# A three-level Strassen-Winograd mixture of experts on one core: P7 and P4 in stages of their own, P4 split a third time

## The chip, the cores and the metric

The kernel runs on one core of one Trainium2 chip. The metric is device time in microseconds (us) of one execution; lower is better. Times are the median of several executions. Beside them stands one execution taken with the hardware profiler, which gives the span of the program's instructions and the trace that all rows below come from.

## What is computed

Soft routing over eight experts: every token goes through every expert, and the results are added with the softmax of the router's logits as weights.

```python
probs = softmax(router_logits)                       # (16, 512, 8)
for e in range(8):
    output += probs[:, :, e:e+1] * (x @ expert_weights[e])   # x (16, 512, 512), W[e] (512, 2048)
```

With the weights of a token multiplied into its row of x this is one matrix product: 8192 tokens by (8 experts x 512) by 2048 output columns, in f32 outside. The kernel multiplies in f16 and sums in f32.

## The kernel before

**The outer level.** The 8192 rows are 32 blocks of 256 (`HQ`, line 55). Blocks 2q and 2q+1 (called a and b) make a pair, q = 0 to 15. The contraction is halved into experts 0 to 3 and 4 to 7, the output into two halves of 1024 columns. On these halves the kernel does a Strassen-Winograd product: seven products P1 to P7 for each q in place of eight. The right operands of P1 to P7 are sums of quarters of the expert weights; the left operands are sums of x times probabilities. `left_of` (line 671) says for each product which blocks of x (`xT` in the profile) and of the probabilities (`pT`) it needs, and `Left.make` (line 452) computes the left operand on VectorE, in two halves `k` (pairs of experts), each 128 x 2048 elements: a multiplication (`z<-xT,pT`), for P7 also a second multiplication of the other block (`u<-xT,pT`) and a subtraction (`z<-z,u`), for P6 a subtraction from P5's operand, and for most P3 a subtraction of a kept operand (`z<-z,w`). The kept operand is P6's left operand of the same q, which `keep_z` (line 1116) writes to DRAM (`z_dram`) while it is in use; `ZBlock` (line 494) loads it back, 1 MB, into a buffer of the weights' pool. `KEPT_Z = 14` (line 625): it is kept for q = 0 to 13, and P3 of q = 14 and 15 multiplies twice, like P7.

**The inner level.** Each product is itself a Strassen-Winograd product of halves (128 rows, one pair of experts, 512 columns): seven steps, in the order 1, 5, 6, 2, 7, 3, 4 (`STEPS`, line 353), each of eight matmuls of 128 x 128 by 128 x 512 (`Product.step`, line 572). A step needs the left operand's first half (steps 1, 5), second half (2, 4), a difference `d` (6) or the sum `i` (3, 7). After each step `post` (line 580) moves the result out of PSUM: alone (`post_alone`, mostly ScalarE copies) or on a base (`post_on_base`, line 606: VectorE adds the step's result to a 128 x 512 f32 tile `h` that holds what another product gave). `Base` (line 635) loads such tiles from DRAM; in `product` (line 696) P7's base is what P6 stored, and P4's base is P7's own tiles, `products[7, q].o`, still in SBUF. Each finished quarter of a product goes to the output by a DMA of GpSimd; P4 and P3 accumulate there (`accum_op=ADD`).

**The third level.** `by_thirds` (line 764) takes steps 1 and 5 of both products of a stage together and does them as one more Strassen-Winograd product: 2 x 7 parts of four matmuls of 128 x 128 by 128 x 256 in place of four steps of eight matmuls by 128 x 512. It needs sums of the two left operands (`Thirds.make`, four VectorE operations of 128 x 1024) and of the weights of steps 1 and 5 (`third_sums`, line 178, eight VectorE operations). Before the change it is used in stages 1 to 3 (P1) and 48 to 54 (P3).

**The order.** `add` (line 657) lines up stages of two products; a stage runs the steps of its two products by turns, and a slot is one step of one product. The list, by index: 0 to 14 P1 and P2; 15 to 30 P5 and P6 (16 alone); 31 (`k7`) P6 15 and P7 0; **32 to 46 P4 q with P7 q+1**; 47 (`k3`) P4 15 and P3 14; 48 to 54 pairs of P3; 55 P3 15.

`run` (line 827) walks through a stage slot by slot. Functions hung at (stage, slot) by `at` are called there: loads of bases (`fetch_at`), of weights (`turnover`, line 1096, on ScalarE's DMA queue), of kept operands (`load_z`, line 1122), and the preparation of P3's weights in four parts (`by_parts`). The other loads of a stage (x, probabilities, kept operands) are put on SyncE's (SP) queue two stages ahead, by `start_loads(stage + 2)` after slot `late.get(stage, 1)`: after the first slot of the stage unless `late` says otherwise; `late` has an entry for stages 46 and 47 only. The next stage's left operands join VectorE's list after slot `wait_for.get(stage, 1)`; they and the weights' sums are done between the additions on PSUM, as far as a cost model in the code (`slack`, line 384) sees room. All instructions of an engine run in the order in which they were issued, and so do the DMA issues of a queue; a DMA issue waits for its tile to be free and for the semaphore it will count on.

**Pools.** 15 buffers for weights and kept operands (8 KB a partition), 12 of 128 x 512 f32 (`h`), 10 for x and probabilities, 6 + 2 banks of PSUM (`ps`, `pt`).

Of the kernel before, what the change touches and what calls it, by code (L numbers as in the profile page):

```python
# [31 lines left out]
def kernel(  # L32
# [477 lines left out]
    class Thirds:  # L510


        def __init__(self, a, b, weights, room=None):
            self.a, self.b, self.weights, self.room = a, b, weights, room
            self.s, self.task = {}, None
# [109 lines left out]
    KEPT_Z = 14  # L625
# [45 lines left out]
    def left_of(r, q, fresh=True):  # L671
        a, b = 2 * q, 2 * q + 1
        if r == 1:
            pt = PBlock(a, P1, xp1[q - 2][1] if q in (2, 3) else None)
            if q in (2, 3):
                xs[a] = XBlock(a, xp1[q - 2][0])
            return Left(xblock(a), pt), [xblock(a), pt]
        if r in (2, 4):
            h, pt = (a, PBlock(a, P2)) if r == 2 else (b, PBlock(b, P2))
            return Left(xblock(h), pt), [xblock(h), pt]  # L680
        if r == 5:
            pt = PBlock(b, PQ)
            return Left(xblock(b), pt), [xblock(b), pt]
        if r == 6:
            pt = PBlock(a, P1)
            return Left(xblock(a), pt, of=lefts[5, q]), [xblock(a), pt]
        if r == 3 and q < KEPT_Z:
            pt, kept_z = PBlock(a, P2), ZBlock(q)
            return Left(xblock(a), pt, kept=kept_z), [xblock(a), pt, kept_z]
        pa, pb = PBlock(a, P1 if r == 7 else PQ), PBlock(b, P1 if r == 7 else PQ)  # L690
        return Left(xblock(a), pa, (xblock(b), pb)), [xblock(a), pa, xblock(b), pb]
# [4 lines left out]
    def product(r, q, **how):  # L696
# [18 lines left out]
        elif r == 6:  # L715
            m1 = bases[6, q]

            def base(tn):
                need(m1.task[tn])
                return m1.t[tn]  # L720
            p = Product(right[6], left, to_out(q, 0, 1), base)
        elif r == 7:
            base = bases[7, q] = Base(lambda tn: out_rows(q, 0, 1, tn))
            p = Product(right[7], left, to_out(q, 1, 1), base)
        elif r == 4:
            p = Product(right[4], left, to_out(q, 1, 0, accum_op=ADD), products[7, q].o.__getitem__)
        else:
            p = Product(right[3], left, to_out(q, 0, 1, accum_op=ADD), **how)
# [35 lines left out]
    def by_thirds(stage):  # L764
# [4 lines left out]
        place, keep = {}, {}  # L769

# [7 lines left out]
        for n, (p, r) in enumerate(((1, 1), (5, 1), (1, 5), (1, 6), (5, 6), (5, 5), (1, 2),  # L778
# [11 lines left out]
            if r == 1:  # L790
                keep[p] = half()
# [19 lines left out]
            elif r == 4:  # L811
                act(nc.scalar.copy(place["h", p][:, cols[0]], x))
                if p == 1:
                    some[1].post(1)
        for product in some:
# [58 lines left out]
    for q in range(15):  # L874
        add(product(4, q), product(7, q + 1))
    some = product(4, 15)
    xs.clear()
    k3 = add(some, product(3, KEPT_Z))
    for q in range(0, KEPT_Z, 2):
# [4 lines left out]
    products[4, 15].apart = True  # L884
# [9 lines left out]
    for q in range(16):  # L894
# [7 lines left out]
        for slot, tn in zip((7, 9, 11, 17), INNER):  # L902
            fetch_at(k7 + q - 1 + slot // 14, slot % 14, bases[7, q], tn)
# [187 lines left out]
    by_parts(k7 + 4, 4, 36, 3, cast_part(22), keep_raw, (9, 16))  # L1091
# [18 lines left out]
    turnover(k7, 0, 4, "t4")  # L1110
    turnover(k3 - 1, 1, 3, "b22", 2)

    for q in range(KEPT_Z):
# [8 lines left out]
    def load_z(q):  # L1122
        load = products[3, q].loads[-1]
        load.by_hook = True
        return load.begin
    at(k3 - 1, 10, load_z(0))
    at(k3, 2, load_z(1))
    third3 = {}

    def third_of_p3(p):  # L1130
        def make():
            third3[p] = third_sums(right[3].w[p])
        later(2.76, make)
    at(k3, 3, lambda: third_of_p3(1))
    at(k3, 5, lambda: third_of_p3(5))
    wait_for[k3] = 6
# [39 lines left out]
    for stage in range(k3 + 1, end):  # L1176
        thirds[stage] = Thirds(*(p.left for p in stages[stage]), third3, new_w)
# [42 lines left out]
```

## Time and profile before

| | us |
|---|---|
| median of 3 runs | 1367.95 |
| lowest and highest | 1367.74, 1368.5 |
| the profiled execution | 1368.82 |
| its span | 1367.0 |
| TensorE busy in it | 1359.6 |
| VectorE busy in it | 1124.8 |

PE in the profile is TensorE's matmuls and PEld its weight loads, DVE is VectorE, ACT ScalarE, POOL GpSimd, SP SyncE; SPq and ACTq are the DMA issues on those queues. A row of the groups gives line, engine, operation, the tile written and read, shapes and count, then busy time, the mean of one in ns, and the idle time before it with what ended it. A row of the timeline gives start, duration, and in brackets the idle time before it. A row of the windows gives a stretch, its length, the busy time (and count) of PE, PEld, DVE, ACT and POOL, the granted clock of TensorE as a share of full speed (1.00 throughout), the busy share of the DMA engines and the GB/s. A row of the DMA issues ends with the KB of one and the median us from issue to landing; a row of the DMA queues gives packets, MB and the share of sixteen engines' time (q0 is GpSimd's queue, q1 SP's, q10 ScalarE's). A matmul's record is longer than its pace: the records overlap.

### The profile page before, as it was taken

The page shows a single profiled execution, that of the slowest core. Times are in us where ns is not written, and L with a number is a line of the kernel's source. Part 1 is how long each engine was busy: PE and PEld are TensorE (multiplying, and loading weights), DVE is VectorE, ACT ScalarE, POOL GpSimd, SP SyncE. Part 2 cuts the span into 40 slices and gives each one's busy share as a digit, 9 for nine tenths or more (in the row PEclk, how much of TensorE's full clock was granted, in tenths as well). Part 3 has the DMA queues.
Part 4 walks back from the last instruction along what each step waited for, and adds up shares of the span by engine and source line. Part 5 has one row for each costly group of instructions (what it writes and reads, how often), then busy time and mean ns, then how long its engine had stood idle before and what let it go on. Part 6 is the DMA issues. An engine that isn't in the chain of part 4 may idle for free.

```text
span 1367.0 us, 18181 instructions
## 1 busy us (share of the span) xinstructions
PE 1359.6 (99%) x6630; PEld 645.4 (47%) x6630; DVE 1124.8 (82%) x1358; ACT 207.3 (15%) x397; POOL 411.8 (30%) x652
## 2 busy tenths in 40 slices
PE   9999999999999999999999999999999999999999
PEld 4555444444444444444444444444444444556554
DVE  7868767679789888788887888888889898898884
ACT  3232111100011111111111100000000000223331
POOL 3233233331223343333322112232332422233232
PEclk9999999999999999999999999999999999999999
DMA  9999999999899999999999998888897979999876
GB/s 185 207 246 233 229 254 255 244 294 385 252 309 273 334 343 317 292 277 316 309 302 324 322 399 240 199 237 208 231 265 203 259 184 298 328 306 240 189 122 127
DMA packets 193290, 360.09 MB, mean 263 GB/s; under 512 B 53168, under 2 KB 87216, under 8 KB 187696
## 3 DMA queue, kind: packets, MB, share of 16 engines
q0 software_dynamic: 88688, 185.12, 56.8%
q1 hardware_dynamic: 100480, 145.36, 35.4%
q10 hardware_dynamic: 4032, 28.44, 5.3%
q8 instruction: 52, 0.85, 0.3%
q14 instruction: 38, 0.31, 0.1%
HBM read 214.99 MB, written 171.11 MB: 282 GB/s over the span
## 4 chain that ended last, share of the span: by engine, by line
PE 97%; DMA 3%; POOL 0%; issue 0%; ACT 0%; DVE 0%; ACTq 0%; POOLq 0%; DVEq 0%
PE ps L130 71%; PE pt L130 25%; DMA h<-out_dram 2%; DMA w<-wd 1%; DMA w<-in_expert_weights_dram 1%; POOL w L121 0%; ACT h L614 0%; DVE ps L107 0%; ACT h L1168 0%; ACTq L164 0%; POOL ident L225 0%; POOLq L225 0%; DVEq L107 0%; POOLq L1204 0%
## 5 line engine op out<-in xcount | busy, mean ns | idle before, releaser
L130 PE MATMUL ps<-w,z 128*128 128x512 f16 (+1 forms) x3704 | 812.2, 376 | 0.8 <-DMA w<-wd 0.5
L130 PEld LDWEIGHTS <-z 128*128 128x128 f16 x5336 | 522.0, 98 | 606.2 <-issue 1.7
L121 POOL DMA_DIRECT2D out_dram<-h x380 | 248.8, 679 | 729.4 <-ACT h L614 337.0
L130 PE MATMUL pt<-w,z 128*128 128x512 f16 (+1 forms) x1632 | 357.7, 369 | 0.6 <-DMA w<-in_expert_weights_dram 0.5
L107 DVE TENSOR_TENSOR h<-ps,h 128x512 f32<-128x512 f32 x260 | 176.8, 686 | 120.9 <-PE ps L130 112.3
L107 DVE TENSOR_TENSOR z<-xT,pT 128x2048 f16<-128x2048 f16 x220 | 266.4, 1216 | 8.2 <-issue 7.2
L130 PE MATMUL ps<-w,d 128*128 128x512 f16 x880 | 199.1, 379 | 0.0
L107 DVE TENSOR_TENSOR h<-pt,h 128x512 f32<-128x512 f32 x155 | 105.7, 687 | 53.5 <-PE pt L130 46.7
L130 PEld LDWEIGHTS <-d 128*128 128x128 f16 x880 | 86.1, 98 | 101.7
L107 DVE TENSOR_TENSOR z<-z,d 128x2048 f16<-128x2048 f16 x110 | 132.4, 1215 | 0.0
L107 DVE TENSOR_TENSOR w<-w 128x1024 f16<-128x1024 f16 (+2 forms) x108 | 111.1, 1039 | 3.4 <-DMA w<-wd 1.7
L614 ACT COPY h<-ps 128x512 f32<-128x512 f32 x64 | 37.5, 586 | 486.2 <-PE ps L130 415.5
L601 ACT COPY h<-ps 128x512 f32<-128x512 f32 x90 | 52.7, 585 | 372.4 <-PE ps L130 316.0
L107 DVE TENSOR_TENSOR d<-z 128x1024 f16<-128x1024 f16 x110 | 74.6, 683 | 0.9
L107 DVE TENSOR_TENSOR ps<-ps,h 128x512 f32<-128x512 f32 (+1 forms) x86 | 54.0, 628 | 22.7 <-PE ps L130 18.6
L121 POOL DMA_DIRECT2D wd<-w x86 | 48.3, 585 | 41.6 <-DVE w L107 26.2
L121 POOL DMA_DIRECT2D w<-in_expert_weights_dram x65 | 48.9, 784 | 38.0 <-DMA wd<-w 28.1
L121 POOL DMA_DIRECT2D kept<-h x56 | 30.8, 550 | 60.2 <-DVE h L107 27.3
L597 ACT COPY h<-ps 128x512 f32<-128x512 f32 x65 | 36.7, 598 | 76.8 <-PE ps L130 67.3
L107 DVE TENSOR_TENSOR h<-h 128x512 f32<-128x512 f32 (+2 forms) x69 | 45.0, 674 | 0.6 <-ACT h L601 0.5
L107 DVE TENSOR_TENSOR z<-z,u 128x2048 f16<-128x2048 f16 x36 | 44.1, 1225 | 1.2
L107 DVE TENSOR_TENSOR u<-xT,pT 128x2048 f16<-128x2048 f16 x36 | 43.8, 1216 | 0.0
(72 smaller groups left out, 352.5 us busy)
## 6 DMA issues: line engine op xcount, KB each, us to landing
out_dram<-h POOLq DMA_DIRECT2D x380, 256.0 KB, 6.9
pT<-p_dram SPq DMA_DIRECT2D x126, 256.0 KB, 6.8
w<-wd ACTq DMA_DIRECT2D x27, 1024.0 KB, 9.7
h<-kept SPq DMA_DIRECT2D x100, 256.0 KB, 7.4
xT<-x SPq DMA_DIRECT2D x73, 256.0 KB, 6.7
wd<-w POOLq DMA_DIRECT2D x72, 256.0 KB, 7.5
w<-in_expert_weights_dram POOLq DMA_DIRECT2D x35, 512.0 KB, 10.5
h<-out_dram SPq DMA_DIRECT2D x68, 256.0 KB, 5.3
```

The costliest lines, as they stand in the source:

```text
L107: dve(nc.vector.tensor_tensor(out=o, in0=a, in1=b, op=op))
L121: note(nc.gpsimd.dma_start(out=o, in_=i, **how))
L130: note(nc.tensor.matmul(ps, z, w, start=start, stop=stop, skip_group_check=True))
L597: act(nc.scalar.copy(o[tn], q if p == 5 else x))
L601: act(nc.scalar.copy(o[TN[p]], b if p == 2 else x))
L614: act(nc.scalar.copy(o[tn], b))
```

## The change

P7 and P4 no longer share stages: 31 is P6 15 with P7 0, 32 to 38 are pairs of P7, 39 (`k4`) is P7 15 with P4 0, 40 to 46 are pairs of P4, 47 is P4 15 with P3 0, 48 to 54 pairs of P3 and 55 P3 15. The number of stages stays.

P4 loads its base from DRAM, from what P7 stored, instead of taking P7's tiles; the bases of both products of a stage are loaded at slots 8, 10 and 12 of the stage before and slot 3 of its own. Stages 40 to 46 use `by_thirds`; as their products lie on a base, the first addition of the second product is moved behind the split's last sum, and two temporary tiles (`keep`) come from the weights' pool.

P6's left operand is kept for all 16 q. P7 of q = 1 to 15 and all P3 use it: block b times its second probabilities minus the kept operand for P7. P7's kept operands of q = 1 and 2 are loaded at slots 0 and 2 of stage 31, as P3's of q = 1 and 2 at the same slots of stage 47; both stages have `wait_for` 6. P4's weights are loaded from stage 38 on, every second slot, instead of every third from stage 30 on; the preparation of P3's weights begins two stages earlier.

```diff
-        if r == 3 and q < KEPT_Z:
-            pt, kept_z = PBlock(a, P2), ZBlock(q)
-            return Left(xblock(a), pt, kept=kept_z), [xblock(a), pt, kept_z]
-        pa, pb = PBlock(a, P1 if r == 7 else PQ), PBlock(b, P1 if r == 7 else PQ)
+        if (r, q) != (7, 0):
+            h = a if r == 3 else b
+            pt, kept_z = PBlock(h, P2), ZBlock(q)
+            return Left(xblock(h), pt, kept=kept_z), [xblock(h), pt, kept_z]
+        pa, pb = PBlock(a, P1), PBlock(b, P1)
...
-            p = Product(right[4], left, to_out(q, 1, 0, accum_op=ADD), products[7, q].o.__getitem__)
+            base = bases[4, q] = Base(lambda tn: out_rows(q, 1, 1, tn))
+            p = Product(right[4], left, to_out(q, 1, 0, accum_op=ADD), base)
...
+        kept = left.keep and left.keep()
...
-                keep[p] = half()
+                keep[p] = half() if kept is None else kept.pop()
...
-                if p == 1:
+                if p == 1 and some[1].base is None:
                     some[1].post(1)
+            if (p, r) == (5, 3) and some[1].base is not None:
+                some[1].post(1)
...
-    for q in range(15):
-        add(product(4, q), product(7, q + 1))
+    for q in range(1, 15, 2):
+        xs.clear()
+        add(product(7, q), product(7, q + 1))
+    some = product(7, 15)
+    xs.clear()
+    k4 = add(some, product(4, 0))
+    for q in range(1, 15, 2):
+        xs.clear()
+        add(product(4, q), product(4, q + 1))
     some = product(4, 15)
     xs.clear()
-    k3 = add(some, product(3, KEPT_Z))
-    for q in range(0, KEPT_Z, 2):
+    k3 = add(some, product(3, 0))
+    for q in range(1, 15, 2):
         add(product(3, q), product(3, q + 1))
...
-        for slot, tn in zip((7, 9, 11, 17), INNER):
-            fetch_at(k7 + q - 1 + slot // 14, slot % 14, bases[7, q], tn)
+    fetch_base = zip((7, 9, 11, 17), INNER)
+    for slot, tn in fetch_base:
+        fetch_at(k7 - 1 + slot // 14, slot % 14, bases[7, 0], tn)
+    for r, q in [(7, q) for q in range(1, 16)] + [(4, q) for q in range(16)]:
+        k = {7: k7, 4: k4}[r] + (q + 1) // 2
+        for slot, tn in zip((8, 10, 12, 17), INNER):
+            fetch_at(k - 1 + slot // 14, slot % 14, bases[r, q], tn)
...
-    by_parts(k7 + 4, 4, 36, 3, cast_part(22), keep_raw, (9, 16))
+    by_parts(k7 + 2, 4, 36, 3, cast_part(22), keep_raw, (9, 16))
...
-    turnover(k7, 0, 4, "t4")
+    turnover(k4 - 1, 1, 4, "t4", 2)
...
-    for q in range(KEPT_Z):
+    for q in range(16):
         z_dram[q] = dram.tile([P, 2 * K8, HQ], f16, name=f"z_{q}")
...
-    at(k3 - 1, 10, load_z(0))
-    at(k3, 2, load_z(1))
...
-    at(k3, 3, lambda: third_of_p3(1))
-    at(k3, 5, lambda: third_of_p3(5))
-    wait_for[k3] = 6
+    for r, k in ((7, k7), (3, k3)):
+        at(k, 0, load_z(r, 1))
+        at(k, 2, load_z(r, 2))
+        wait_for[k] = 6
+    for r, k in ((4, k4), (3, k3)):
+        at(k, 3, lambda r=r: make_third(r, 1))
+        at(k, 5, lambda r=r: make_third(r, 5))
...
-    for stage in range(k3 + 1, end):
-        thirds[stage] = Thirds(*(p.left for p in stages[stage]), third3, new_w)
+    def keep_in_w():
+        t = wpool.tile([P, 4, NB], f32, name="keep", tag="w")
+        return [t[:, 0], t[:, 1]]
+    for r, first, to, keep in ((4, k4 + 1, k3, keep_in_w), (3, k3 + 1, end, None)):
+        for stage in range(first, to):
+            thirds[stage] = Thirds(*(p.left for p in stages[stage]), third_of[r], new_w, keep)
```

More of the change, by code (lines that the diff above doesn't have):

```diff
@@ L510, with __init__ @@
     class Thirds:
-        def __init__(self, a, b, weights, room=None):
-            self.a, self.b, self.weights, self.room = a, b, weights, room
+        def __init__(self, a, b, weights, room=None, keep=None):
+            self.a, self.b, self.weights, self.room, self.keep = a, b, weights, room, keep
             self.s, self.task = {}, None
@@ L624 @@
     QK = 9
-    KEPT_Z = 14
     ND = QK // 2
@@ L883 @@
     late[k3] = 10
-    products[4, 15].apart = True
     def claim(of, tn):
@@ L1120, with load_z, make_third @@
         at(k, 5, lambda keep_z=keep_z: keep_z(1))
-    def load_z(q):
-        load = products[3, q].loads[-1]
+    def load_z(r, q):
+        load = products[r, q].loads[-1]
         load.by_hook = True
         return load.begin
-    at(k3 - 1, 10, load_z(0))
-    at(k3, 2, load_z(1))
-    third3 = {}
-    def third_of_p3(p):
+    third_of = {4: {}, 3: {}}
+    def make_third(r, p):
         def make():
-            third3[p] = third_sums(right[3].w[p])
+            third_of[r][p] = third_sums(right[r].w[p])
         later(2.76, make)
-    at(k3, 3, lambda: third_of_p3(1))
-    at(k3, 5, lambda: third_of_p3(5))
-    wait_for[k3] = 6
+    for r, k in ((7, k7), (3, k3)):
[5 more added lines that the diff above has]
+        at(k, 5, lambda r=r: make_third(r, 5))
     finish = products[3, 15]
```

## The prediction, made before the changed kernel ran

> **What bounds the kernel now.** I read the head of the profile and the shares of its chain first, then the matmuls in order of time.
>
> ```profile
> span 1367.0 us, 18181 instructions
> ...
> PE 1359.6 (99%) x6630; PEld 645.4 (47%) x6630; DVE 1124.8 (82%) x1358; ACT 207.3 (15%) x397; POOL 411.8 (30%) x652
> ...
> PE 97%; DMA 3%; POOL 0%; issue 0%; ACT 0%; DVE 0%; ACTq 0%; POOLq 0%; DVEq 0%
> ```
>
> TensorE is busy for 99% of the span and makes 97% of the chain, so time is gained by fewer matmul columns and lost by holes between matmuls. I call the entries of `stages` by their index: 31 is (P6 15, P7 0), 32 to 46 the mixed pairs, 47 (P4 15 and a P3), 48 to 54 the P3 pairs with the third split.
>
> ```profile
> 828.24 3.62 PE L130 MATMUL pt<-w,z 128*128 128x512 f16 x16
> ...
> 852.41 3.62 PE L130 MATMUL pt<-w,z 128*128 128x512 f16 x16
> ```
> ```profile
> 1257.78 1.04 PE L130 MATMUL pt<-w,z 128*128 128x256 f16 x8
> ...
> 1281.16 1.04 PE L130 MATMUL pt<-w,z 128*128 128x256 f16 x8
> ```
>
> The first two rows are the same step of two successive mixed stages: 24.17 us for 14 steps of 8 matmuls, so 1.727 us a step (a slot, below) and 0.2159 us a matmul. The other two are the starts of two successive P3 stages with the third split: 23.38 us. Holes inside the part that changes:
>
> ```profile
> 796.01 7.07 PE L130 MATMUL ps<-w,z 128*128 128x512 f16 x32
> 802.92 3.62 PE L130 MATMUL pt<-w,z 128*128 128x512 f16 x16
> 806.37 3.62 PE L130 MATMUL ps<-w,d 128*128 128x512 f16 x16
> 809.83 5.34 PE L130 MATMUL ps<-w,z 128*128 128x512 f16 x24
> 815.49 1.89 PE L130 MATMUL ps<-w,z 128*128 128x512 f16 x8 [0.32 <-DVE h L107]
> 817.21 3.62 PE L130 MATMUL pt<-w,z 128*128 128x512 f16 x16
> 821.32 2.98 PE L130 MATMUL ps<-w,z 128*128 128x512 f16 x13 [0.49 <-DMA w<-wd]
> ```
>
> Twenty-four matmuls from 809.83 end at 815.01, but the next starts at 815.49 (0.48 late); sixteen from 817.21 end at 820.66, the next starts at 821.32 (0.66 late). That is 1.14 us in stage 32, where P4's weights arrive beside everything else. Two slots before 802.92 stage 32 begins: 799.47; stage 31 begins 14 slots earlier, at 775.29.
>
> **The change part by part.**
>
> *Third split of P4.* Stages 40 to 46 hold seven P4 pairs. If each runs like a P3 pair, TensorE saves 7 x (24.17 - 23.38) = **-5.53 us**. VectorE must follow:
>
> ```profile
> L107 DVE TENSOR_TENSOR z<-xT,pT 128x2048 f16<-128x2048 f16 x220 | 266.4, 1216 | 8.2 <-issue 7.2 <-DMA xT<-xs 1.0
> L107 DVE TENSOR_TENSOR z<-z,w 128x2048 f16<-128x2048 f16 x28 | 34.3, 1224 | 1.0
> L107 DVE TENSOR_TENSOR h<-ps,h 128x512 f32<-128x512 f32 x260 | 176.8, 686 | 120.9 <-PE ps L130 112.3
> L107 DVE TENSOR_TENSOR d<-z 128x1024 f16<-128x1024 f16 x110 | 74.6, 683 | 0.9
> ```
> ```profile
> 849.00:873.10 24.10, 24.10 (x113) 10.92 (x112) 20.43 (x24) 1.17 (x2) 5.60 (x9) 1.00 0.75 187
> 1257.78:1281.16 23.38, 23.38 (x137) 13.30 (x136) 20.55 (x26) 8.23 (x18) 7.28 (x9) 1.00 0.95 230
> ```
>
> (The fourth number of a row is VectorE's busy time, the last the GB/s.) A P3 pair multiplies and subtracts a kept operand (8 long operations); a P4 pair only multiplies (4), but its two products lie on a base: 12 adds of 0.686 us instead of 4. So -4 x 1.22 + 8 x 0.686 = +0.6 us on 20.55, under 23.38: no steady limit. PSUM's turn at the end of the split's fourteen parts gets one add of 0.69 us where P3 has a ScalarE copy; the next matmul on that bank is one part and one slot (0.43 + 1.73 us) away. I cost it at 0, and at up to 0.8 us a pair if the add comes late. The eight subtractions for P4's third weights (of `d`'s size, 0.68 each) fall in stage 39, with the four sums for stage 40's left operands and four long operations fewer than a mixed stage has: 20.43 + 12 x 0.68 - 4 x 1.22 = 23.7 of 24.17 us. Hidden, just.
>
> *P7 pairs.* A P7 had multiply, multiply, subtract for each half; now it has multiply and subtract of the kept operand. A stage of two P7 has 8 long operations, two `d`, two `z<-z,d` and 12 adds: as many as the mixed stage's 24 (20.43 us). Nothing on TensorE.
>
> *P4's weights leave stages 31 and 32.* They move to stages 38 and 39 with at least 13 slots between the last slot that gates each load and its use (22 us or more), as P3's weights have in stages 46 and 47, which show no hole. The 1.14 us goes: **-1.14 us**. What is late next is below.
>
> *DMA.* Rows of the page:
>
> ```profile
> out_dram<-h POOLq DMA_DIRECT2D x380, 256.0 KB, 6.9
> pT<-p_dram SPq DMA_DIRECT2D x126, 256.0 KB, 6.8
> w<-wd ACTq DMA_DIRECT2D x27, 1024.0 KB, 9.7
> ...
> h<-out_dram SPq DMA_DIRECT2D x68, 256.0 KB, 5.3
> ```
>
> A P7 stage now puts 14 transfers on SP: 2 `xT`, 2 `pT`, 8 bases (256 KB each) and 2 kept operands (1024 KB), 5.24 MB; with 8 stores (2.1 MB) and about 0.9 MB for P3's weights it moves 8.2 MB in 24.17 us, 340 GB/s. Stages of before that moved as much:
>
> ```profile
> 461.00:485.20 24.20, 24.20 (x113) 10.94 (x112) 21.87 (x29) 3.50 (x6) 10.33 (x20) 1.00 1.04 358
> 775.30:799.50 24.20, 24.20 (x114) 10.98 (x113) 21.24 (x26) 1.76 (x3) 4.32 (x8) 1.00 1.01 373
> 799.50:824.80 25.30, 24.49 (x114) 10.86 (x113) 20.27 (x24) 1.17 (x2) 5.41 (x8) 1.00 1.04 388
> ```
>
> 358 GB/s went without a hole; 388 had holes. In steady P7 stages bases are issued more than 13 slots ahead, so I cost them at 0. The Trainium skill, "DMA: Bandwidth & Descriptors", section Specifications, puts what HBM gives one core at about 358 GB/s. The third row is above it, so the measurement decides; by the rule the 24.2 us at 373 GB/s would take 25.2, 1 us more (an estimate).
>
> *Entry into P7 (stage 31): the new wait.* Stage 32 needs the kept operands z1 of (P7 1) and z2 of (P7 2). Their loads hang at slots 0 and 2 of stage 31, and between them stage 33's loads are put on SP at slot 1 (for stage 47 the code delays these to slot 10; for 31 nothing does). SP's order is z1, x, p, z3, x, p, z4, **z2**, bases. All of it stands behind a base that today goes out with the second of these:
>
> ```profile
> 770.30 5.27 SPq L118 DMA_DIRECT2D h<-out_dram  x2
> ```
> ```profile
> 782.98 0.58 ACT L601 COPY h<-ps 128x512 f32<-128x512 f32 x1 [17.26 <-DMA out_dram<-h]
> 783.00 2.22 ACTq L164 DMA_DIRECT2D w<-wd  x4
> ```
>
> So z1 goes out at about 775.5. z2 has one more gate: by the new program's waits it needs P7's sixth weight (step 3) landed. That load stands on ScalarE's queue behind the copy that a store holds until 783. Loads of that kind:
>
> ```profile
> w<-wd ACTq DMA_DIRECT2D x1, 1024.0 KB, 7.0
> ```
> ```profile
> w<-z SPq DMA_DIRECT2D x1, 1024.0 KB, 10.5
> ```
> ```profile
> q1 hardware_dynamic: 1224, 4.13, 51.1%
> ...
> w<-z SPq DMA_DIRECT2D x5, 1024.0 KB, 15.4
> ```
> ```profile
> w<-z SPq DMA_DIRECT2D x1, 1024.0 KB, 17.6
> ```
>
> The first row is the weight issued at 783 alone (a window around it). With z traffic beside it I take 8 us: landed, and z2 issued, at 791. A kept operand takes from 10.5 us (issued at 1165, little ahead of it) over a median of 15.4 (five of them between 1174 and 1197, `xT` and `pT` between) to 17.6 (issued at 1190.4). z2 has 2 MB of z3 and z4 and four small loads ahead, like the five; next to plain stores, not accumulating ones, I take 14.5. **z2 lands at 805.5** (801.5 to 808.6).
>
> Behind it VectorE has, in its order: subtract (1.22), three adds (0.69), `d` (0.68), multiply and subtract (2.44), two adds (1.38), some 7.8 us, 7.3 with the overlap seen between operations (24 operations of 21.8 us are 20.43 busy). The last of these adds frees the bank on which (P7 1) goes on in slot 4 of stage 32: 799.47 + 4 x 1.727 = 806.4. z2 would have to land by 799.1; it is 6.4 us late: **+6.4 us** (2.4 to 9.5). Bases queued behind z2 follow within the shifted time.
>
> And a stretch (1156 to 1166) with weights and kept operands on the way together, by queue, packets and MB:
>
> ```profile
> q10 hardware_dynamic: 296, 2.20, 57.6%
> q1 hardware_dynamic: 133, 1.04, 26.3%
> ```
>
> The same skill page, section Queues, rings and completion order, says that each DMA engine takes turns between the queues packet by packet; by it a kept operand would move at the pace of a weight, and z2 be nearer to the 10.5 us. The trace agrees in part only: the weights' queue (q10) moved 2.20 MB there, SP's (q1) 1.04.
>
> *Sum.* -5.53 - 1.14 + 6.4 = -0.3 us. The profiled execution took 1368.82 us around a span of 1367.0, 0.87 over the median of 1367.95; the difference carries over: 1367.95 - 0.3 = **1367.7 us**.
>
> **The rivals.**
>
> *The entry costs little* (faster). If z2 lands by about 802, stage 32 loses under 4 us, and the time is 1367.95 - 6.67 + (0 to 4) = 1361.3 to 1365.2. For it: 10.5 us is in the trace, and stage 47, with the same kind of entry, has no hole. Against: there z2's counterpart had one operand ahead of it, here three.
>
> *SP does not keep up in the P7 stages* (slower). They need 5.24 MB in 24.17 us from SP's queue, 217 GB/s. Between 1174 and 1197 that queue (q1) moved 4.13 MB in 23 us, 180 GB/s, while its loads queued up. It decides below 217: at 208 a stage takes 25.2 us, +1.0 for each of stages 32 to 38, and with the entry 1367.7 + 7 = 1375; at 180 it would be far more. Against: those stores accumulate, P7's do not, and the 358 GB/s row has no hole.
>
> *The split does not give P4 what it gives P3*: the add in place of the copy comes late in each pair, 0.8 us x 7 = 5.5 us, 1373.3. Against: VectorE's sum above.
>
> **How the numbers follow.** Forecast 0.47 (own range 1365.2, where the cheap entry begins, to 1370.8, z2 at its latest), entry cheap 0.27, SP too slow 0.20, split no gain 0.06. A measurement of this kernel tells about 0.2% (2.7 us) from no change, so the forecast is "within" (1365.2 to 1370.7): faster 0.27, same 0.47, slower 0.26. Range 1362.5 to 1374.5: below it lies the lowest part of the cheap entry (0.05), above it most of what a slow SP would be (0.13).
>
> **What would show it.** Right: stages 40 to 46 at 23.38 us; stage 32 stretched by 4 to 9 us with TensorE waiting for VectorE, and VectorE's subtraction waiting for DMA `w<-z` until about 805; no hole in stages 34 to 39. Wrong: stage 32 within 2 us of 24.17 (z2 in time), every P7 stage longer by the same amount (SP's rate), or P4 pairs at 24 us.

## The result and the profile after

The changed kernel takes **1378.79 us** (median of 6 executions, 1377.25 to 1383.66) beside 1368.14 of the kernel before (6 executions, 1367.74 to 1369.15): a ratio of 1.0082, 95% interval 1.0067 to 1.0098. It is 0.8% slower, and lies above the range of the prediction. The profiled execution took 1383.66 us, 4.9 over the median, so the holes below are probably somewhat larger than those of a usual execution.

The head, the chain and four DMA rows of the page after:

```profile
span 1381.9 us, 18753 instructions
...
PE 1361.0 (98%) x6798; PEld 663.5 (48%) x6798; DVE 1121.4 (81%) x1388; ACT 227.4 (16%) x453; POOL 411.7 (30%) x652
...
PE 71%; issue 15%; DMA 9%; POOL 5%; DVE 0%; SPq 0%; POOLq 0%; ACT 0%; ACTq 0%; DVEq 0%
...
out_dram<-h POOLq DMA_DIRECT2D x380, 256.0 KB, 7.8
h<-out_dram SPq DMA_DIRECT2D x132, 256.0 KB, 11.2
w<-z SPq DMA_DIRECT2D x31, 1024.0 KB, 14.0
...
w<-wd ACTq DMA_DIRECT2D x27, 1024.0 KB, 9.5
```

VectorE does no more than before, and TensorE's part of the chain fell from 97% to 71%. The base loads are 64 more, and one takes 11.2 us to land instead of 5.3. The times between the first matmuls of successive stages tell where the span grew. Each row below is a stage's length less 24.17 us (23.38 with the third split); what is not listed ran to within 0.3 us of that.

| kernel (profiled execution) | 31 | 32 | 38 | 39 | 43 | 46 | 47 | others |
|---|---|---|---|---|---|---|---|---|
| before | | 1.15 | | | | | | |
| after | | 5.74 | 1.18 | 7.79 | 2.16 | 4.17 | | |

The other stages with P4's split, 40 to 42, 44 and 45, last exactly 23.38 us, and 33 to 37 24.17. So the split gave what was forecast, and 21 us of holes took it back: 21.04 - 5.53 - 1.15 = 14.4 of the spans' 14.9; the other 0.5 lies ahead of stage 31, which the change does not touch.

TensorE's rows at the four large holes:

```profile
805.89 3.41 PE L130 MATMUL ps<-w,z 128*128 128x512 f16 x8 [4.06 <-DVE z L107]
```
```profile
995.32 5.97 PE L130 MATMUL ps<-w,z 128*128 128x512 f16 x16 [4.17 <-DVE h L107]
```
```profile
1093.34 10.53 PE L130 MATMUL ps<-w,z 128*128 128x512 f16 x48 [1.99 <-DVE z L107]
```
```profile
1161.08 3.29 PE L130 MATMUL ps<-w,d 128*128 128x512 f16 x8 [2.60 <-DVE ps L107]
```

It waits for VectorE each time, so the next view is what VectorE waited for: in stage 32 for the kept operand z2; in stages 38 (the first row of the second view), 39 (the next four) and 43 (the last two) for bases.

```profile
804.60 1.23 DVE L107 TENSOR_TENSOR z<-z,w 128x2048 f16<-128x2048 f16 x1 [9.55 <-DMA w<-z]
```
```profile
960.99 0.69 DVE L107 TENSOR_TENSOR h<-pt,h 128x512 f32<-128x512 f32 x1 [4.93 <-DMA h<-out_dram]
...
979.44 0.69 DVE L107 TENSOR_TENSOR h<-ps,h 128x512 f32<-128x512 f32 x1 [2.50 <-DMA h<-out_dram]
...
982.09 0.70 DVE L107 TENSOR_TENSOR ps<-ps,h 128x512 f32<-128x512 f32 x1 [0.82 <-DMA h<-out_dram]
...
985.05 0.70 DVE L107 TENSOR_TENSOR ps<-ps,h 128x512 f32<-128x512 f32 x1 [1.14 <-DMA h<-out_dram]
...
990.38 0.69 DVE L107 TENSOR_TENSOR h<-pt,h 128x512 f32<-128x512 f32 x1 [1.75 <-DMA h<-out_dram]
...
1087.61 0.69 DVE L107 TENSOR_TENSOR h<-ps,h 128x512 f32<-128x512 f32 x1 [1.15 <-DMA h<-out_dram]
...
1090.13 0.69 DVE L107 TENSOR_TENSOR h<-ps,h 128x512 f32<-128x512 f32 x1 [1.24 <-DMA h<-out_dram]
```

Stage 46 is another matter. VectorE first, then ScalarE and its queue:

```profile
1160.33 0.70 DVE L107 TENSOR_TENSOR ps<-ps,h 128x512 f32<-128x512 f32 x1 [3.54 <-DMA pT<-p_dram]
```
```profile
1159.51 0.33 ACTq L164 DMA_DIRECT2D w<-wd  x1
1159.94 0.63 ACT L814 COPY ps<-pt 128x256 f32<-128x256 f32 x2 [6.27 <-DMA xT<-x]
```

VectorE's row names a load of p, but that load was still on its way until 1163.0. What came just before 1160.33 was the first of the two ScalarE copies of line 814, which the split needs; the trace has VectorE's add wait for its semaphore. The copies stood 6.27 us behind a load of P3's weights on ScalarE's queue, and this load could be issued only when a load of x that counts on the same semaphore had landed (1159.5). No base is in that chain.

SP's queue around stages 38 and 39, first its own rows, then what its issues waited for from 925 to 1000 us (us in total, times, longest):

```profile
963.21 18.34 SPq L118 DMA_DIRECT2D h<-out_dram  x8
```
```profile
SPq L118 <- DMA h<-out_dram: 30.8, 13, 5.3
SPq L118 <- DMA out_dram<-h: 20.7, 5, 8.3
```

Eight base loads took SP 18.34 us to issue. It waited 20.7 us for stores to land (`out_dram<-h`: the tile `h` that a base is to fill still holds the result of an earlier step) and 30.8 us for base loads (the transfer before it on the same semaphore). And the loads, once issued, are slow; the DMA issues of stage 38:

```profile
h<-out_dram SPq DMA_DIRECT2D x6, 256.0 KB, 16.4
w<-in_expert_weights_dram POOLq DMA_DIRECT2D x4, 256.0 KB, 16.4
```

The second row is one of the four parts of P3's weights, cast from f32 on their way by GpSimd's queue, which begins in stage 38.

**Theory A** (on record for 46 as well): 12 tiles `h` do not suffice. Each base claims its tile from load to store, 8 tiles a stage; where landings are long, a store lands late, so the next base goes out late. **The rivals**: the third split's own order of additions makes the holes of 43 and 46 (C); the parts of P3's weights alone make those of 38 and 39 (G); SP or the DMA engines as a whole are full. Apart from it, stage 32 is the order on SP (E) or a gate that no order opens (F).

### The profile page after: what moved, and what is told of

The parts are those of the page before. It is cut to its first block, busy times and chain, and to the rows that moved or that the text cites. A ratio compares the mean times of both kernels' runs of the same rounds, so it can differ in the third digit from the quotient of the medians.

```text
span 1381.9 us, 18753 instructions
## 1 busy us (share of the span) xinstructions
PE 1361.0 (98%) x6798; PEld 663.5 (48%) x6798; DVE 1121.4 (81%) x1388; ACT 227.4 (16%) x453; POOL 411.7 (30%) x652
## 4 chain that ended last, share of the span: by engine, by line
PE 71%; issue 15%; DMA 9%; POOL 5%; DVE 0%; SPq 0%; POOLq 0%; ACT 0%; ACTq 0%; DVEq 0%
PE ps L130 53%; PE pt L130 17%; POOL out_dram L121 4%; DMA out_dram<-h 4%; DMA w<-in_expert_weights_dram 2%; DMA w<-z 1%; DMA w<-wd 1%; POOL wd L121 1%; DMA pT<-p_dram 1%; DMA wd<-w 0%; POOL w L121 0%; SPq L118 0%; POOLq L121 0%; DVE z L107 0%; DVE h L107 0%
## 5 line engine op out<-in xcount | busy, mean ns | idle before, releaser
L130 PE MATMUL ps<-w,z 128*128 128x512 f16 (+1 forms) x3760 | 823.9, 376 | 11.1 <-DVE z L107 6.0
L130 PE MATMUL pt<-w,z 128*128 128x512 f16 (+1 forms) x1520 | 322.7, 360 | 0.3 <-DMA w<-in_expert_weights_dram 0.3
L107 DVE TENSOR_TENSOR h<-ps,h 128x512 f32<-128x512 f32 x288 | 195.0, 687 | 125.9 <-PE ps L130 111.0
L107 DVE TENSOR_TENSOR h<-pt,h 128x512 f32<-128x512 f32 x127 | 86.4, 687 | 44.4 <-PE pt L130 32.8
L107 DVE TENSOR_TENSOR w<-w 128x1024 f16<-128x1024 f16 (+2 forms) x116 | 116.3, 1016 | 3.9 <-DMA w<-wd 2.1
L107 DVE TENSOR_TENSOR z<-z,w 128x2048 f16<-128x2048 f16 x62 | 76.0, 1225 | 12.0 <-DMA w<-z 10.0
L107 DVE TENSOR_TENSOR ps<-ps,h 128x512 f32<-128x512 f32 (+1 forms) x86 | 54.1, 630 | 27.3 <-PE ps L130 16.4
L130 PEld LDWEIGHTS <-w 128*128 128x128 f16 x528 | 49.2, 99 | 8.1 <-DMA w<-in_x_dram 1.5
## 6 DMA issues: line engine op xcount, KB each, us to landing
h<-out_dram SPq DMA_DIRECT2D x132, 256.0 KB, 11.2
```

The lines of the kernel that those rows point to most:

```text
L107: dve(nc.vector.tensor_tensor(out=o, in0=a, in1=b, op=op))
L130: note(nc.tensor.matmul(ps, z, w, start=start, stop=stop, skip_group_check=True))
```

## The experiments

Rows are profiled executions as above; the medians stand in the text, with the 95% interval of the ratio to the kernel before.

| kernel | 31 | 32 | 38 | 39 | 43 | 46 | 47 | others |
|---|---|---|---|---|---|---|---|---|
| stage 33's loads later | | 5.44 | 1.94 | 4.40 | 4.44 | 1.85 | | |
| no split of P4 | | 6.65 | 0.42 | 5.33 | | | | 48: 0.64 |
| P4 without base loads | | 7.25 | | 2.14 | | | | |
| 14 `h`, 8 for x | 7.62 | 1.17 | | 0.61 | | | | 2: 7.37, 10: 0.71, 20: 0.41 |
| 14 `h`, 10 for x | | 6.26 | | | | | 1.31 | 48: 0.76 |
| (P7 2) twice | 7.10 | 1.05 | | 6.36 | 5.68 | 1.45 | | |
| 14 `h`, (P7 2) twice | | 1.94 | | | | | 0.51 | 30: 0.60, 48: 0.76 |
| 14 `h`, order | | | | 1.62 | | | 1.12 | 20: 0.82, 48: 0.76 |
| 14 `h`, order, parts in 40 to 45 | | | | | | 12.83 | | 42: 10.89, 45: 5.50, 44: 2.07, 41: 1.51, 20: 0.92, 48: 0.47, 19: 0.38 |
| parts in 40 to 45 alone | | 6.95 | | | | 8.34 | | 42: 13.43, 45: 8.76, 41: 1.51, 44: 0.65, 48: 0.46 |
| before with 14 `h` | | 3.91 | | | | | | 26: 1.21 |
| 14 `h`, order, parts every 44 | | | | | | | 0.28 | 20: 1.80, 19: 0.95 |
| the same, P7's sums later | 4.10 | | | | | 2.72 | 3.45 | 22: 1.83, 21: 1.60, 30: 1.26, 26: 0.67 |

**1. Stage 33's loads behind z2.**

```diff
+    late[k7] = 10
```

> The changed kernel with stage 33's loads put on SP's queue at slot 10 of stage 31 instead of slot 1, so that z2 goes out ahead of z3 and z4. Theory A (the entry is late because z2 has three kept operands' worth of loads ahead of it on SP; the holes of stages 38, 39, 43 and 46 are another matter, the bases' cycle): stage 32's 5.7 us shrink to under 1.5, the other four stages keep their holes, 1373 to 1375 us. Rival (z2 is late because its weight gate opens late, whatever the order): stage 32 keeps over 4 us, 1377 to 1379. Rival (SP as a whole is behind in every P7 stage): what 32 gives back comes up in 33 to 38, 1378.

1381.66 us (1.0079 to 1.0109). z2 was in time now: the subtractions of kept operands ran at 794.99 and 800.17. But stage 32 kept its hole; VectorE waited for a base in place of z2:

```profile
812.99 1.37 DVE L107 TENSOR_TENSOR h<-pt,h 128x512 f32<-128x512 f32 x2 [7.53 <-DMA h<-out_dram]
```

The edit put z3 and z4 between the bases of slot 8 and those of slot 10. So it was not z2 alone: whatever stands behind those 2 MB is late. The other holes changed their sizes but not their places, and the median did not gain. My expectation of 1373 to 1375 failed.

**2. P4 without the third split.**

```diff
-    for r, k in ((4, k4), (3, k3)):
+    for r, k in ((3, k3),):
...
-    for r, first, to, keep in ((4, k4 + 1, k3, keep_in_w), (3, k3 + 1, end, None)):
+    for r, first, to, keep in ((3, k3 + 1, end, None),):
```

The first pair of lines takes out the sums for P4's third weights in stage 39 as well.

> The changed kernel without the third split of P4 (stages 40 to 46 do their 14 steps of eight matmuls; P4 still on a base from DRAM). Theory A (bases cycle): 40 to 46 cost 24.17 instead of 23.38, +5.5 us; the holes of 38 and 39 (9 us) stay, those of 43 and 46 (6.3 us) stay at over half, since the same bases, stores and weights move in nearly the same time: 1381 to 1384 us. Rival C (the split's order of adds and its temporary tiles make the holes of 43 and 46): both go, and 39 loses the part that third sums cost, 1374 to 1378.

1381.97 us (1.0082 to 1.0113). The holes of 43 and 46 went, as C has it; 39's stayed. The total is at A's number, though, since the saving of 5.5 went with them. This run alone does not tell C from A: without the split a stage is 0.8 us longer, and the base of a step is needed later after the stage's start. In 46 the copies of line 814 go with the split.

**3. P4 without base loads.** Zeros are added in place of P7's part, which is missing from that quarter of the output; the 64 loads are left out.

```diff
-            base = bases[4, q] = Base(lambda tn: out_rows(q, 1, 1, tn))
-            p = Product(right[4], left, to_out(q, 1, 0, accum_op=ADD), base)
+            p = Product(right[4], left, to_out(q, 1, 0, accum_op=ADD), lambda tn: nil.to_broadcast([P, NB]))
+            p.apart = True
...
-    for r, q in [(7, q) for q in range(1, 16)] + [(4, q) for q in range(16)]:
+    for r, q in [(7, q) for q in range(1, 16)]:
```

> The changed kernel with P4's 64 base loads taken out: VectorE adds a broadcast column of zeros instead, in as many additions of the same size, so that P7's part is missing from that quarter of the output. A base's buffer is then claimed at the first addition, not at the load. Theory A (base loads and their buffers): the holes of 43 and 46 go (6.3 us), and of 38 and 39 more than half (5 to 8 of 9 us), 1365 to 1368 us. Rival C (the split and VectorE's order): holes stay, 1377 to 1379. Rival D (weight turnover and P3's weights on the DMA engines in 38, 39 and 46): 43 goes, 39 and 46 stay at over half, 1372 to 1376.

1374.75 us (1.0031 to 1.0074), and above the expected 1365 to 1368, for stage 32 kept 7.25 us. With the split and as many additions, the holes of 38, 43 and 46 are gone: C falls for 43. (In 46 the copies ran 5.0 us after the stage's start, in after 9.5.) What is left in 39 is a P4 weight:

```profile
989.26 3.63 PE L132 MATMUL ps<-w,z 128*128 128x512 f16 x16 [1.24 <-DMA w<-wd]
```

**4. 14 tiles, taken from x.**

```diff
-    xpool = ctx.enter_context(tc.tile_pool(name="xpool", bufs=10))
-    hpool = ctx.enter_context(tc.tile_pool(name="hpool", bufs=12))
+    xpool = ctx.enter_context(tc.tile_pool(name="xpool", bufs=8))
+    hpool = ctx.enter_context(tc.tile_pool(name="hpool", bufs=14))
```

> The changed kernel with 14 tiles of 128x512 f32 for bases and results instead of 12, and 8 instead of 10 for x and probabilities. Theory A, buffer form (a base load waits until the store that used its buffer has landed): two more buffers are a quarter of a stage, 6 us, more lead: holes of 39, 43 and 46 (14 us) shrink to under 5, 1368 to 1371 us, if the loads of x keep up. Rival, DMA form (the loads go out in time and land late, since the DMA engines are full): holes stay within 2 us, 1377 to 1380; with x late too, more.

1377.38 us (1.0047 to 1.0081), above the 1368 to 1371 of the buffer form, which held only for the holes: from 38 to 46 all but 0.61 us went. Stages 2 and 31 lost 15 us instead; around 31 (765 to 825 us) SP waited for tiles that VectorE still read:

```profile
SPq L118 <- DVE z L107: 14.2, 4, 12.6
```

**5. 14 tiles, x left alone.** The 4 KB tile `u` is given up; its contents go through two `h` tiles, by halves.

```diff
-    hpool = ctx.enter_context(tc.tile_pool(name="hpool", bufs=12))
+    hpool = ctx.enter_context(tc.tile_pool(name="hpool", bufs=14))
...
-                u = new_u()
-                times(u, k, *self.less)
-                tt(t, t, u, SUB)
+                for e in range(2):
+                    u, half_ = h_tile([P, C, HQ], f16), t[:, ds(e * C, C)]
+                    tt(u, xb.t, pb.t[:, ds(2 * k + e, 1)].to_broadcast([P, C, HQ]), MUL)
+                    tt(half_, half_, u, SUB)
...
```

> The changed kernel with 14 tiles of 128x512 f32 and the 10 tiles for x and probabilities left as they are; the room comes from the separate 4 KB tile u, whose contents (GpSimd-stored weights, and the subtrahend of (P7 0)) now pass through two such tiles each, by halves. Theory A, buffer form: as with 14 and 8, the holes of 38, 39, 43 and 46 (15.3 us together) fall below 2, and stage 2 and 31 no longer wait for x; stage 32 keeps 5 to 7: 1364 to 1367 us. Rival (it was the delay at stage 31 by late x that spread the loads, not the buffers): holes of 39 to 46 come back at over 8 us, 1372 to 1378.

1369.65 us (0.9996 to 1.0015), 9 us under the changed kernel. From 33 to 46 no hole of 0.3 us is left: A is shown for 38, 39 and 43. (In 46 the copies ran 5.0 us after the stage's start, as in run 3.) The time stands 2.7 us above the expected 1364 to 1367: stage 32 lost what was expected, but 47 and 48 lost 2.07 us that were not. SP's waits from 925 to 1000 us:

```profile
SPq L118 <- DMA h<-out_dram: 21.7, 14, 3.8
...
SPq L118 <- DMA out_dram<-h: 4.3, 3, 3.4
```

Waiting for stores fell from 20.7 us to 4.3. How far ahead of its use a base goes out can be worked out from its issue and the slot that needs it (us, the eight bases of stage 39 in the order of their loads):

```
after      ahead  11.5 12.8 12.1 12.4  5.4  5.5  4.3  4.5   landing 15.4 17.9 17.2 19.4 14.8 14.8  4.7  3.8
14 tiles   ahead  23.9 21.2 19.7 21.0 20.7 21.0 22.5 23.3   landing 13.3 12.5 10.7 11.7 11.2 11.5 17.5 20.6
```

The landings are not much shorter. They are covered.

Why two tiles do so much can be worked out from the code. Tiles are taken in turn, so with 12 a base gets the tile of the twelfth base before it. For the third pair of a stage (slot 12; the fifth and sixth number of a row) that is the first pair of the stage before, which is stored after slots 6 and 7. The third pair is needed after slots 4 and 5 of its own stage, 12 slots or 20.7 us later, and between the two the store must land, the base go out, and the base land. In after this pair went out 0.1 us after that store had landed in each of stages 34 to 40 but 38. In stage 39 the stores took 10.1 and 8.9 us and the bases 14.8 each: 24.9 and 23.7 of 20.7 us. The other pairs have 18 slots, but stand in the same queue. With 14 tiles every pair has 20 slots, 34.5 us.

**6. and 7. (P7 2) multiplied twice, so that z2 is not loaded; alone and with 14 tiles.**

```diff
-        if (r, q) != (7, 0):
+        if r == 3 or q not in (0, 2):
...
-        at(k, 2, load_z(r, 2))
+        if r == 3: at(k, 2, load_z(r, 2))
```

> The changed kernel with (P7 2) multiplied twice instead of subtracting z2, so that stage 31 loads one kept operand for stage 32 and no wait for a weight's landing stands before the bases on SP. Theory E (the entry is late because everything on SP behind the weight-gated z2 and the 1 MB loads is late, bases included: taking z2 away brings the bases of stage 32 forward by the 9 us that SP stood): stage 32 loses under 2 us instead of 5.7, plus at most 1 for VectorE's longer list, 1374 to 1376. Rival F (the bases of stage 32 wait for stores and buffers anyway): stage 32 keeps over 4 us, 1377 to 1379.

> Both: 14 tiles as above and (P7 2) multiplied twice. Theory A with E: only small holes are left, 1360 to 1364 us, under the kernel before. Theory A with F (the entry stays): as the 14 tiles alone.

Alone 1381.08 us (1.0076 to 1.0108), above both expectations: stage 32 falls to 1.05, as E has it, but its hole comes up in stage 31, where a weight of P7 is late:

```profile
803.59 8.05 PE L130 MATMUL ps<-w,z 128*128 128x512 f16 x24 [5.28 <-DMA w<-wd]
```

With 14 tiles 1368.68 us (0.9992 to 1.0011). The profiled execution (1365.58) was its fastest; the median is 5 us over what was expected.

**8. 14 tiles, and stage 33's loads behind stage 32's bases.**

The edit stands on that of run 5.

```diff
...
+    late[k7] = 14
...
+    wait_for[k7 + 1] = 6
```

> 14 tiles as above, with z2 kept, stage 33's loads put on SP after slot 13 of stage 31, behind the bases of slots 8 to 12, and stage 33's left operands put on VectorE's list after slot 6 of stage 32. If the entry is a matter of order on SP alone, both z2 and the bases are in time and stage 32 loses under 2 us, but z3 and z4 come 20 us later than now and stage 33 may pay up to 3: 1360 to 1364. If the entry is set by the DMA rate (SP has 2 x 1 MB, weights and bases to move in the same 25 us in whatever order), stages 32 and 33 lose 4 to 7 together: 1364 to 1368.

1368.53 us (0.9988 to 1.0013). Stages 31 to 33 have no hole at all, against 6.26 us with 14 tiles alone: with 14 tiles the entry was a matter of order (E), of z2 and of the bases together, not of the DMA rate. The median still lies above the 1360 to 1364 that went with it. The executions spread from 1364.5 to 1372.0. In the profiled one 39 lost 1.62, with a P4 weight late by 1.44:

```profile
993.78 1.90 PE L130 MATMUL ps<-w,z 128*128 128x512 f16 x8 [1.44 <-DMA w<-wd]
```

A P7 stage of it, 34, as a window (columns as in the prediction), shows 395 GB/s beside a busy TensorE:

```profile
847.70:871.90 24.20, 24.20 (x114) 10.94 (x112) 21.75 (x27) 1.17 (x2) 6.99 (x13) 1.00 1.03 395
```

**9. and 10. The parts of P3's weights moved into stages 40 to 45; with all of 8, and alone.**

```diff
-    by_parts(k7 + 2, 4, 36, 3, cast_part(22), keep_raw, (9, 16))
+    by_parts(k4 + 1, 4, 16, 3, cast_part(22), keep_raw, (9, 16))
```

> 14 tiles and stage 33's loads behind stage 32's bases, as in the last run, and the preparation of P3's weights moved from stages 33 to 42 into stages 40 to 45 (every 16 slots from slot 4 of stage 40), where 240 to 290 GB/s were moved instead of 330 to 395. Theory A: the last hole of stages 38 and 39 (1.6 us, a P4 weight that lands late) goes, only 47 and 48 keep about 1.9, and with less traffic in 33 to 39 the executions scatter less: 1362.5 to 1365.5 us, under the kernel before. Rival (P4's own weights on ScalarE's queue are late for another reason): 39 keeps its hole, 1364 to 1368.5.

> The changed kernel with 12 tiles and its own order, and only the preparation of P3's weights moved to stages 40 to 45. Theory A (buffer cycle; the parts' traffic only lengthens the landings): 38 and 39 lose 9 us less 2 to 5, 43 and 46 gain nothing or lose 1 to 3 more: 1374 to 1380. Rival G (the parts in 38 and 39 are the cause of those holes): 38 and 39 under 1.5, 1369 to 1372.

1397.98 us (1.0184 to 1.0235) and 1406.26 us (1.0236 to 1.0289): far off. With a part begun every 16 slots, VectorE waited in its order for the store of a raw part, which its sums overwrite:

```profile
1068.28 2.87 DVE L107 TENSOR_TENSOR w<-w 128x1024 f16<-128x1024 f16 x4 [6.62 <-DMA wd<-w]
```

But the second kernel answers G, for 38 and 39. With 12 tiles and nothing else changed they have no hole, where A alone had 4 to 7 us left, and a base lands in 6.2 us instead of 16.4 (950.7 to 974.9, after's stage 38; this kernel's begins 0.8 us later):

```profile
DMA packets 2788, 8.37 MB, mean 346 GB/s; under 512 B 376, under 2 KB 376, under 8 KB 2409
...
h<-out_dram SPq DMA_DIRECT2D x8, 256.0 KB, 6.2
```

The same window of the changed kernel:

```profile
DMA packets 3411, 7.92 MB, mean 327 GB/s; under 512 B 352, under 2 KB 1367, under 8 KB 3091
...
q0 software_dynamic: 1512, 2.47, 46.7%
```

It moved less, at 327 GB/s, and a base took almost three times as long. So it was not the bytes: the casting loads made the landings long. They put 1015 packets of 512 B to 2 KB into the window that without them has none, and GpSimd's queue (q0) held the engines for 46.7% of the time to move 2.47 MB (without them 24.1% for 2.18); that it is the size of these packets is argued from this, not shown. Other stages of after agree: in 33 and 41, each with four casting loads, a base took 13.9 and 12.9 us, in 34 and 40, which moved more GB/s without them, 10.1 and 8.2.

The bases of this kernel's stage 39, as in the table of run 5, and one row of SP's waits from 925 to 1000 us:

```
parts late ahead  18.8 19.6 20.8 21.5 14.4 10.9 19.7 16.1   landing  6.2  6.0  6.2  6.0  8.5  8.5  8.9  4.3
```
```profile
SPq L118 <- DMA out_dram<-h: 45.3, 11, 8.2
```

SP waited more than twice as long for stores as in after (20.7 us), and nothing was lost: the wait of a queue is no cost as long as the lead that is left covers the landing. So it takes both to make the holes of 38 and 39, too few tiles and long landings, and either remedy is enough: short landings with 12 tiles, or 14 tiles with long ones. For 43, 14 tiles, no base loads, or the longer stage without the split each were.

**11. The kernel before with 14 tiles.** The same tiles and the same halves for `u`.

> The kernel before with 14 tiles in place of 12, u taken apart in the same way (a P7's subtrahend is made and subtracted by halves, four operations of 128x1024 in place of two of 128x2048). Theory A: it had no hole for want of tiles, so nothing is gained, and up to 1.5 us lost by VectorE's extra operations: 1367 to 1370. If tiles were short there too, its 1.4 us of holes go: 1366.5.

1372.52 us (1.0009 to 1.0034). More tiles bring the kernel before nothing; it loses 2.8 in stage 32 (3.91 for 1.15) and 1.2 in 26. That is more than I had expected. In stage 32 VectorE waited 5.13 us for a base (at 805.06); why that base was late stays open.

**12. 14 tiles, order, and the parts every 44 slots**, so that none begins in stage 38 or the first half of 39.

```diff
-    by_parts(k7 + 2, 4, 36, 3, cast_part(22), keep_raw, (9, 16))
+    by_parts(k7 + 2, 4, 44, 3, cast_part(22), keep_raw, (9, 16))
```

> 14 tiles, stage 33's loads behind stage 32's bases, and the four parts of P3's weights started every 44 slots from slot 4 of stage 33 instead of every 36, so that they start in stages 33, 36, 39 (slot 8) and 42 and none lies in stage 38 and the first half of 39, where P4's weights are loaded. Theory: the loads of 38 and 39 land some us sooner and the 1.6 us that 39 waited for a P4 weight go: profile with holes in 47 and 48 only, 1362.5 to 1365.5 us for the profiled execution, the median 1364 to 1368. Rival: the loads of the fourth part in 42 and 43 cost there what they cost in 39, 1367 to 1371; or stage 20 and other places outside the change, which showed holes of up to 0.9 with this set of tiles, decide the scatter, and the median stays at 1368.5.

**1365.79 us** (median of 11, 1363.91 to 1370.98), ratio 0.9983, 0.9973 to 0.9994: the one version that beats both kernels. Three windows of its profile, stages 31, 39 and 43, columns as in the prediction:

```profile
778.33:802.50 24.17, 24.17 (x113) 10.98 (x112) 20.18 (x25) 1.76 (x3) 4.32 (x9) 1.00 1.02 411
...
971.70:995.90 24.20, 24.20 (x114) 10.95 (x113) 22.53 (x32) 1.17 (x2) 8.33 (x12) 1.00 1.04 330
...
1066.03:1089.41 23.38, 23.38 (x138) 13.30 (x136) 21.14 (x29) 4.09 (x10) 8.57 (x11) 1.00 1.09 248
```

TensorE is busy throughout. From 31 to 46 there is no hole. The time came as expected, but not all of the mechanism: the holes that were left lay not in 47 and 48 but in 19 and 20, outside the change, 2.75 us. In 20 VectorE waited 3.96 us for a load that the sums of P7's weights need (at 530.66); in 19 it was busy up to the hole. Without the two the span would be 1361.0.

**13. The same, with those sums 10 slots behind their loads instead of 7.**

```diff
-    by_parts(k5 + 2, 4, 13, 7, load_part("t3"), None, (7,))
+    by_parts(k5 + 2, 4, 13, 7, load_part("t3"), None, (10,))
```

> As the last run, with the sums of P7's weights (stages 17 to 20) put on VectorE's list 10 slots after each part's load instead of 7. If the 2.75 us that stages 19 and 20 lost in the last run's profile are VectorE waiting for these loads, with additions that free TensorE's banks queued behind, both holes go: a profiled execution at 1361.5 to 1363.5 us, the median 1362 to 1365.5. The sum of the prediction's steps without an entry was 1361.3. Rival (the holes there are the cost of 14 tiles, whose base loads go out earlier and stand against the parts; they move to another wait): 19 and 20 lose over 1 us, 1364.5 to 1366.5.

1377.37 us (1.0033 to 1.0072; 1369.92 to 1379.29). The holes of 19 and 20 went and came back in 21 and 22, and the profiled execution had holes in 31, 46 and 47 that the run before had not. Why a shift in stages 17 to 20 is felt in 46 was not settled. The rival, that these holes move, was the nearer one, and even it was too low.

## Why the prediction was wrong, by its own steps

- **Third split, -5.53 us: right.** Seven stages of P4 at 23.38 us, in after those five without a hole, in run 12 all seven. The add in the copy's place cost nothing, and the sums for the third weights fit into stage 39 (run 12). The rival without a gain falls.
- **P7 pairs, nothing: right.** Stages 33 to 37 last 24.17 us.
- **P4's weights, -1.14 us and no new hole: half right.** The old hole went. "As P3's weights have in stages 46 and 47" did not hold: a P4 weight ended a wait of 1.24 us in run 3 and of 1.44 in run 8. In after itself no matmul waited for one: the bases were later. And P3's weights, the model for it, had a hole in stage 46 this time (below).
- **DMA, "bases are issued more than 13 slots ahead, so I cost them at 0": the step that failed.** In the profiled execution it should have been 11.1 us, the holes of 38, 39 and 43. I read the lead from the order of the program, where nothing holds SP's issue but its place. In the trace a base waits for the store that empties its tile: 13 slots are 22.5 us, and stage 39's bases went out 4.3 to 12.8 us ahead, with landings of up to 19.4. By the code the third pair's tile is stored only 12 slots, 20.7 us, before its use (run 5). With the page's medians, 6.9 us for a store and 5.3 for a base, that still looks like nothing; with the landings of a busy stretch it does not, and before's trace had one: of what was issued between 786 and 794 us, a store took 8.3 and a base 17.7 (medians), 26 us in all.
- **Stage 46, 4.17 us: a wait that the sum did not have.** The prediction looked at the split's turn on PSUM by VectorE's add alone, and took P3's weights in stage 46 as harmless, as they were before. With the split in 46, VectorE needs ScalarE's copies early in the stage, and these stand behind the weights' loads on ScalarE's queue. Run 1 shows the same: the copies waited 5.36 us there, and 46 lost 1.85.
- **The rival "SP does not keep up in every P7 stage": wrong in place and cause.** 33 to 37 had no hole, though they moved up to 364 GB/s, and stage 34 of run 8 moved 395 without one. The loss stood where landings were longest (the bases of 38 and 39 took 15.7 and 15.1 us, medians; those of the other stages from 32 to 46, 8.3 to 12.9) and in 43, one of the stages that the split shortens.
- **The rule on what HBM gives one core, weighed there:** the Trainium skill, "DMA: Bandwidth & Descriptors", section Specifications, about 358 GB/s. The trace disagrees: 411 over the 24.17 us of stage 31 in run 12, with TensorE busy throughout.
- **Entry, +6.4 us (2.4 to 9.5): right in size, right only in part in its mechanism.** 5.74 us, and z2 used at 804.60 where I had it landing at 805.5; the cheap entry, under 4, falls. The nearness to 6.4 is in part luck: z2 made TensorE 4.2 us late, and the other 1.5 are matmuls at half pace (below), which the sum did not have. And TensorE stopped already at slot 1, for the left operand of (P7 2) itself, not at slot 4 for a bank. Besides, the entry was no matter of z2 alone: with z2 early the bases behind it cost as much (run 1), with z2 gone a weight did (run 6).
- **Holes cost more than their length.** I priced a hole by its idle time. After three of after's four large holes TensorE went on at half pace, which is 5.1 of the 21 us (below).
- **What would show it:** the signs for the split and for stage 32 came as written; against "no hole in stages 34 to 39" spoke 38 and 39, and for 43 and 46 no sign had been named.

The gains were forecast at 6.67 us. Run 12 shows them without most of the holes: its span of 1363.7 less 3.0 of holes against 1367.0 less 1.4 (1.15 in stage 32, 0.26 in 49) is a gain of 4.9, and before's hole of 1.15 in stage 32 is gone as well, 6.1 together. What turned the sum were the holes of 38, 39, 43 and 46, 15.3 us in the profiled execution, 11.1 of them by bases, that the forecast had at nothing. In a usual execution, whose time is 4.9 us less, they are probably smaller.

## What to carry to other kernels

When a change takes a tile's contents through DRAM instead of keeping them in SBUF, multiply it out: tiles of the pool, over tiles used in a stage, times the stage's length is the round of one tile, and it must hold the load's landing, the use and the store's landing, all at the durations of the busiest stretch and not at the page's median. Then look for the tile with the least time between its store and its next use: here two of a stage's eight had 12 slots, the others 18. A lead read from program order is only a lead if the buffer is free by then. Loads that an engine issues between its own work can hold up that work, as ScalarE's copies in stage 46. And how long a transfer takes is read from who else is on the DMA engines at that moment: here a base took 16.4 us beside casting loads and 6.2 without them, at more GB/s.

## What the runs showed of the hardware

**The clock falls after a hole.** In after's stage 39 sixteen matmuls from 995.32 took until 1001.12, 5.80 us in place of 3.45; their starts were 0.427 us apart for eleven matmuls, then 0.216. The window's granted clock (last but two):

```profile
976.07:1008.03 31.96, 26.85 (x113) 11.56 (x112) 23.56 (x33) 1.07 (x2) 7.02 (x11) 0.89 0.96 344
```

Over all runs, starts up to 2.6 us apart, away from a longer hole, were not followed by it; of twelve between 2.9 and 4.2 us some were (2.98 in after) and some not (3.74 in run 1); of those from 4.37 on, all were. The Trainium skill, "TensorE: Matmul & The Clock Gate", Part 1, has a free-running window of about 3.4 us of activity that decides on half or full rate. The runs agree with that. The trace's records of the granted clock give the stretches at half clock: in after they begin at 805.56, 993.30 and 1160.55 us, 55 and 49 times 3.413 us apart, and last 3.41, 6.83 and 3.41 us, and in every run with several of them they begin a whole number of such steps apart. Where a hole of 3 to 4 us falls in such a window decides whether it costs 1.4 to 2.8 us more. It may be some of the spread of the executions.
